# Which engine forms the low parts in the run-up to sparse attention, and when the compressed values of that layer are formed

## The chip, the cores and the metric

The kernel runs on one core of a Trainium2 chip. The metric is the device time of one execution in microseconds (us). Before the change the median of three runs is 1415.6 us (1414.58 to 1415.69). The trace comes from one more execution, which took 1416.84 us and whose span, from its first to its last instruction, is 1415.1 us.

## The reference, cut to what matters

The program is a two-layer decoder trunk over 512 tokens of width 1024. Layer 0 mixes retention and mLSTM heads. Layer 1 is a sparse-attention mixer. Each layer is followed by a gated feed-forward part and by an embedding of its own that is gated and added. Only the mixer of layer 1 matters here:

```
z = (h @ w_in).astype(jnp.float32)
q, kc, vc, ks, vs, kw, vw, gt = split_cols(z, NSA_SIZES)
q = rms_norm(q.reshape(B, T, G, HG, HD), q_g).transpose(0, 2, 3, 1, 4)
...
def compress(t, pos, w1, w2):
    blk = kv(t)[:, cidx] + pos[:, None, :]
    blk = blk.transpose(0, 3, 1, 2, 4).reshape(B, G, nc, CMP_BLOCK * HD)
    return jax.nn.gelu(blk @ w1) @ w2

kc = rms_norm(compress(kc, pos_k, w1k, w2k), k_g[0])
vc = compress(vc, pos_v, w1v, w2v)
```

There are 16 query heads of width 64. Keys and values are compressed in overlapping blocks of 32 tokens by a two-layer network: w1 (2048 to 256), a gelu, then w2 (256 to 64). "The second layer of the compressed values" is the product with w2 for the values. Scores against the compressed keys, against the selected blocks and against the window are then turned into probabilities, and their products with the values are added with gates. The layer's embedding `p @ ple_w` doesn't depend on the mixer and is worked in among the attention steps.

## The kernel before, in words

**Products in three pieces.** Every product of f32 data is done with each operand split into a high and a low part. ScalarE (ACT) copies the source to the high part (line 133), another engine subtracts it from the source for the low part (line 134), and TensorE (PE) runs three matmuls into one accumulator: high by high (L152), high by low (L153 or L154) and low by high (L154 or L153).

**Weights.** `load` (line 136) brings in one weight tile of 128x1024 f32, 512 KB. SyncE (SP) issues its DMA into `wr`, ACT forms `wh`, and either VectorE (DVE) or GpSimd (POOL) forms `wl`. Which of the two is read off the string `lo_seq`: "v" is DVE, "g" is POOL, and after each load the string is rotated by one letter, so that "vg" alternates. `wr`, `wh` and `wl` have three buffers each, so the fourth tile after a given one takes over its buffers once it is used up. `load` runs with a raised priority (`AHEAD` = 500 places), so the planner puts a tile's DMA, its `wh` and its `wl` far ahead of their place in the program.

**Order.** A planner goes over the traced program and writes one fixed queue for each engine from priorities and modelled costs. On the chip each engine works its queue in order, and semaphores hold an instruction until its inputs are there. Nothing overtakes on an engine.

**The run-up to attention**, from line 958 on, in program order: `thin` (two tiles w_cmp, the sum of squares and the scale of the norm), `kv` (four tiles w_kv), `blocks` and `kv_evac` (keys and values out of PSUM, the norm of the keys on DVE, their gains on POOL at L701), `hidden(0)` (four tiles w1, matmuls L745, L746 and L748), the first half of the queries `q0` (four tiles w_q, 24 three-piece matmuls each) with `key_stack` in between (transposes L714), the second layer of the compressed keys, `q_norm` of the first query halves on DVE (L818 to L831), `hidden(1)`, `q1` (four tiles w_q), and between the third and fourth tile of `q1` first `cmp_values(second(1, ...))` and then four `q_stack` (16 transposes at L838). After the fourth tile come four more `q_stack`, then `cmp_scores` (L858 to L870), and then the attention loop. That makes 22 loads: 2 + 4 + 4 + 4 + 4 + 4, and "vg" gives 11 of them to POOL.

**The attention loop** runs scores (L899 to L901), the maximum on DVE (L902), the exponential on ACT (L904), the division and gate on POOL (L909), transposes (L921) and products with the values (L931 to L943). Other work is hung into its steps: the embedding of the layer (`Embed.step`, three loads: pT and the first half of w_ple at m = 0, the second half at m = 4), the second half of the queries' norm on POOL, and the first half of the output projection (four loads of w_nso). `lo_seq` is "g" for all seven loads, so POOL forms 18 low parts in this layer's mixer.

`cmp_values` writes `vc`, which the first product at L931 reads. It takes two copies of 64 columns on ACT (L802), two subtractions on DVE (L803) and two products of 128x512 on DVE (L805). `second(1)` takes 12 matmuls of 128x64 (lines 152 to 154).

Of the kernel before, what the change touches and what calls it, by code (L numbers as in the profile page):

```python
# [60 lines left out]
class Trunk:  # L61
# [553 lines left out]
    def nsa_mixer(self):  # L615
# [4 lines left out]
        with ExitStack() as ctx:  # L620
# [134 lines left out]
            def hidden_t(hid, times):  # L755
                pt = self.ps("b")
                for q in range(2):
                    nc.tensor.transpose(pt[:, 64 * q : 64 * q + 64], hid[0:64, P * q : P * q + P], self.ident[0:64, 0:64])
                hh, hl = [self.y()[:, 0 : P * times].rearrange("p (x r b) -> p x r b", x=4, b=32) for _ in range(2)]
                self.split(hh, hl, pt[:, 0:P].rearrange("p (x b) -> p x b", x=4).unsqueeze(2).to_broadcast([P, 4, times, 32]))  # L760
                return hh, hl


            def second(which, hh, hl):
                po = self.ps("o")
                for g in range(1 + which):
                    out = po[:, 64 * g : 64 * g + 64] if which else po[0:64, 0:64]
                    for q in range(2):
                        ws = slice(P * which + 64 * q, P * which + 64 * q + 64)
                        xs = slice(2 * q + g, 2 * q + g + 2 - which)  # L770
                        ah, al = [x[:, xs].rearrange("p x r b -> p (x r b)") for x in (hh, hl)]
                        self.mm3(out, ah, al, w2[:, 0, ws], w2[:, 1, ws], q == 0, q == 1)
                return po
# [24 lines left out]
            def cmp_values(po):  # L798
                tmp = self.sc()
                for g in range(2):  # L800
                    hi, lo = tmp[:, P * g : P * g + 64], tmp[:, P * g + 64 : P * g + P]
                    nc.scalar.activation(hi.bitcast(F32R), po[:, 64 * g : 64 * g + 64], AF.Copy)  # L802
                    nc.vector.tensor_tensor(lo, po[:, 64 * g : 64 * g + 64], hi, ALU.subtract)  # L803
                    both = tmp[:, P * g : P * g + P].unsqueeze(1).to_broadcast([P, 4, P])
                    nc.vector.tensor_tensor(vc[g], both, rows4.unsqueeze(2).to_broadcast([P, 4, P]), ALU.mult)  # L805
# [29 lines left out]
            def q_stack(sts, hd):  # L835
                pk = self.ps("b")
                for t in range(NTT):
                    nc.tensor.transpose(pk[:, t * P : (t + 1) * P], sts[t][hd // 4][:, hd % 4].bitcast(F32).rearrange("p a d -> p (a d)"), self.ident)  # L838
                q = self.y()
                if hd % 2:  # L840
                    nc.vector.tensor_copy(q, pk)
                else:
                    nc.scalar.activation(q, pk, AF.Copy)
                return q


            def cmp_scores(g, qs):
                es = []
                for jp in range(2):
                    e = self.sc()  # L850
                    e4 = e.rearrange("p (j h n) -> p j h n", j=2, h=8)
                    e3 = e.rearrange("p (h n) -> p h n", n=32)
                    mx, sm = self.small(16), self.small(16)
                    for jj in range(2):
                        j = 2 * jp + jj
                        ps = self.ps("b").rearrange("p (h a n) -> p h a n", h=8, a=2)
                        for q in range(8):
                            nc.tensor.matmul(ps[:, q], qs[q][:, j * P : (j + 1) * P], kc[:, :, 32 * g : 32 * g + 32], start=True, stop=True)  # L858
                        nc.vector.tensor_tensor(e4[:, jj], ps[:, :, 0], maskc[:, j].unsqueeze(1).to_broadcast([P, 8, 32]), ALU.add)
                        nc.vector.tensor_tensor(e4[:, jj], e4[:, jj], ps[:, :, 1], ALU.add)  # L860
                    nc.vector.tensor_reduce(mx, e3, AX, ALU.max)
                    nc.gpsimd.tensor_tensor(e3, e3, mx.unsqueeze(2).to_broadcast([P, 16, 32]), ALU.subtract)
                    nc.scalar.activation(e, e, AF.Exp)
                    nc.vector.tensor_reduce(sm, e3, AX, ALU.add)
                    nc.vector.reciprocal(sm, sm)
                    sm3 = sm.rearrange("p (j h) -> p j h", j=2)
                    nc.vector.tensor_tensor(sm3, sm3, gate[:, 2 * jp : 2 * jp + 2, 8 * g : 8 * g + 8, 0], ALU.mult)
                    if jp == 0:
                        nc.vector.tensor_scalar(sm[:, 0:8], sm[:, 0:8], valid, None, ALU.mult)
                    nc.gpsimd.tensor_tensor(e3, e3, sm.unsqueeze(2).to_broadcast([P, 16, 32]), ALU.mult)  # L870
                    es.append(e)
                return es
# [82 lines left out]
                    outs[g][0].append(hi)  # L955
                    outs[g][1].append(lo)

            self.lo_seq = "vg"
            w2r = self.sc()
            nc.sync.dma_start(w2r[:, 0:256], I["w2"])  # L960
            w2 = np_.tile([P, 2, 256], F32R, name="w2")
# [27 lines left out]
            hvt = hidden_t(hv, 4)  # L989
            cmp_keys_t(st)  # L990
            q1.steps(2, 3)
            cmp_values(second(1, *hvt))
            qs = [q_stack(sts, hd) for hd in range(4)]
            q1.steps(3, 4)
            qs += [q_stack(sts, hd) for hd in range(4, 8)]
            ess = [cmp_scores(0, qs), None]
            self.lo_seq = "g"
            sts1 = []
            zq = [q_copy(q1.ps[0:2], 0), q_copy(q1.ps[2:4], 2)]

# [7 lines left out]
            emb = self.Embed(self, 1, lambda m: self.y().bitcast(F32))  # L1008

            def embed(m):  # L1010
                return lambda: emb.step(m)

            def more_q(lo, hi):
                def run():
# [18 lines left out]

            hooks[3] = [set_probs(0)]
            at("embed", [embed(m) for m in range(KD)])
            at("q_stack", [more_q(2 * i, 2 * i + 2) for i in range(4)])
            at("q_norm", [lambda i=i: q_norm(zq[i], sts1, nc.gpsimd) for i in range(2)])
# [241 lines left out]
```

## Time and profile before

| | |
|---|---|
| median of three runs | 1415.6 us |
| the profiled execution | 1416.84 us, span 1415.1 us |
| PE matmul busy | 1374.4 us, 97% |
| DVE busy | 847.2 us, 60% |
| ACT busy | 637.9 us, 45% |
| POOL busy | 383.2 us, 27% |
| mean granted clock of PE | 0.992 |

An engine's busy time is the time in which it has an instruction in work. A granted clock of 1.00 is 2.4 GHz and 0.5 is 1.2 GHz. A row of the waits says which instruction waited for which, how long in total, how often and at most. In the timelines a row is the start, the duration, the engine, the line, the operation and what it writes and reads. What stands in brackets is the engine's idle time before the instruction and what ended it. Matmuls overlap in the pipeline, so the rate is read from start to start and not from their durations.

### The profile page before, as it was taken

The numbers are of one execution on the slowest core, as the hardware profiler recorded it, in microseconds if no ns is written. First come the engines' busy times: TensorE is split into PE (matmuls) and PEld (weight loads), VectorE is DVE, ScalarE is ACT, GpSimd is POOL, SyncE is SP. The second block draws the span as 40 slices with busy tenths as digits, with TensorE's granted clock in tenths as the row PEclk, the third lists the DMA queues.
The fourth block names the chain that finished last, engine by engine and source line by source line (L and its number), as shares of the span: only waits on it lengthen the run. The fifth ranks groups of instructions, "written<-read, shape, count | busy, mean of one in ns | idle before, by whom it ended". The sixth has DMA issues, their size and how long they took to land.

```text
span 1415.1 us, 17986 instructions
## 1 busy us (share of the span) xinstructions
PE 1374.4 (97%) x6726; PEld 1127.8 (80%) x6726; DVE 847.2 (60%) x1368; ACT 637.9 (45%) x1121; POOL 383.2 (27%) x361
## 2 busy tenths in 40 slices
PE   9999999999999999999988899999999999999998
PEld 7778778888888888887766777777888888888887
DVE  6665656565356435577827798777575437534555
ACT  5257426444134223444443787777444224323341
POOL 4466102122041001123233675544222013100120
PEclk9999999999999999999999999999999999999999
DMA  6433323223323333333323110010233323333232
GB/s 215 129 114 92 112 79 107 90 91 104 94 85 105 104 89 93 96 118 96 106 88 119 31 31 30 16 46 5 86 104 98 96 90 105 94 100 94 84 106 75
DMA packets 40031, 127.96 MB, mean 90 GB/s; under 512 B 4740, under 2 KB 5380, under 8 KB 39944
## 3 DMA queue, kind: packets, MB, share of 16 engines
q1 hardware_dynamic: 39656, 126.68, 29.1%
q8 instruction: 53, 0.87, 0.3%
q14 instruction: 34, 0.28, 0.1%
q10 hardware_dynamic: 288, 0.14, 0.0%
HBM read 122.60 MB, written 3.15 MB: 89 GB/s over the span
## 4 chain that ended last, share of the span: by engine, by line
PE 82%; DVE 7%; ACT 3%; issue 3%; POOL 2%; POOLq 0%; ACTq 0%; DVEq 0%
PE ps L153 25%; PE ps L152 25%; PE ps L154 25%; PE ps L921 2%; PE ps L943 2%; ACT pr L904 1%; PE ps L363 1%; ACT pt L133 1%; DVE nmx L902 1%; DVE wl L134 1%; PE ps L900 1%; PE ps L899 1%; DVE pt L134 1%; PE ps L421 1%; DVE tiny L186 1%
## 5 line engine op out<-in xcount | busy, mean ns | idle before, releaser
L152 PE MATMUL ps<-y,wh 128*128 128x512 f32 (+1 forms) x1112 | 434.8, 391 | 3.3 <-ACT y L206 2.2
L153 PE MATMUL ps<-y,wh 128*128 128x512 f32 (+1 forms) x1112 | 432.1, 389 | 0.6 <-POOL y L134 0.6
L154 PE MATMUL ps<-y,wl 128*128 128x512 f32 (+1 forms) x1112 | 431.8, 389 | 0.0
L133 ACT ACTIVATE wh<-wr 128x1024 fp32r<-128x1024 f32 (+2 forms) x223 | 230.0, 1036 | 427.8 <-PE ps L153 347.4
L134 DVE TENSOR_TENSOR wl<-wr,wh 128x1024 fp32r<-128x1024 f32 (+2 forms) x185 | 226.8, 1228 | 48.3 <-ACT wh L133 47.8
L152 PEld LDWEIGHTS ps<-y,wh 128*128 128x128 f32 x1112 | 209.3, 188 | 47.4 <-ACT y L206 2.6
L153 PEld LDWEIGHTS ps<-y,wh 128*128 128x128 f32 x1112 | 209.3, 188 | 43.4 <-POOL y L134 1.1
L154 PEld LDWEIGHTS ps<-y,wl 128*128 128x128 f32 x1112 | 209.1, 188 | 43.3 <-DVE wl L134 0.2
L1082 POOL TENSOR_TENSOR sc<-sc,rb 128x512 f32<-128x512 f32 x44 | 56.9, 1293 | 476.7 <-ACT sc L1081 476.7
L152 PE MATMUL ps<-gh,wh 128*128 128x512 f32 x352 | 136.9, 389 | 0.0
L153 PE MATMUL ps<-gl,wh 128*128 128x512 f32 x352 | 136.9, 389 | 0.0
L154 PE MATMUL ps<-gh,wl 128*128 128x512 f32 x352 | 136.9, 389 | 0.0
L200 POOL TENSOR_TENSOR acc<-acc,sc 128x512 f32<-128x512 f32 x48 | 74.4, 1551 | 218.3 <-ACT sc L198 215.4
L134 POOL TENSOR_TENSOR wl<-wr,wh 128x1024 fp32r<-128x1024 f32 x36 | 88.1, 2449 | 160.9 <-ACT wh L133 140.5
L1097 DVE TENSOR_TENSOR hp<-hp,ps 128x512 f32<-128x512 f32 x48 | 33.0, 687 | 130.4 <-PE ps L154 130.4
L909 POOL TENSOR_SCALAR pr<-pr,sm,gate 128x512 f32<-128x512 f32 (+3 forms) x128 | 77.3, 615 | 65.5 <-DVE sm L907 45.8
L1083 DVE TENSOR_TENSOR sc<-ps,sc 128x512 f32<-128x512 f32 x44 | 30.4, 692 | 92.7 <-POOL sc L1082 83.5
L1075 DVE TENSOR_TENSOR a<-ps,rb 128x512 f32<-128x512 f32 x44 | 30.4, 690 | 91.8 <-PE ps L154 88.9
L152 PEld LDWEIGHTS ps<-gh,wh 128*128 128x128 f32 x352 | 66.1, 188 | 13.8
L153 PEld LDWEIGHTS ps<-gl,wh 128*128 128x128 f32 x352 | 66.1, 188 | 13.7
L154 PEld LDWEIGHTS ps<-gh,wl 128*128 128x128 f32 x352 | 66.1, 188 | 13.6
L1081 ACT ACTIVATE sc<-sc 128x512 f32<-128x512 f32 x44 | 27.8, 632 | 101.3 <-DVE sc L1080 101.3
(284 smaller groups left out, 2038.9 us busy)
## 6 DMA issues: line engine op xcount, KB each, us to landing
wr<-in_w_up_dram SPq DMA_DIRECT2D x88, 512.0 KB, 3.6
wr<-in_w_down_dram SPq DMA_DIRECT2D x32, 512.0 KB, 3.5
wr<-in_w_plg_dram SPq DMA_DIRECT2D x16, 512.0 KB, 3.7
wr<-in_w_down_dram SPq DMA_DIRECT2D x16, 384.0 KB, 3.1
hp<-in_xT_dram SPq DMA_DIRECT2D x16, 256.0 KB, 3.9
wr<-in_w_abo_dram SPq DMA_DIRECT2D x8, 512.0 KB, 3.6
wr<-in_w_dram SPq DMA_DIRECT2D x8, 512.0 KB, 3.7
wr<-in_w_q_dram SPq DMA_DIRECT2D x8, 512.0 KB, 3.7
```

What stands on the lines that cost most here:

```text
L133: self.nc.scalar.activation(hi, src, AF.Copy)
L134: (eng or self.nc.vector).tensor_tensor(lo, src, hi.bitcast(F32), ALU.subtract)
L152: mm(out, ah, bh, start=first, stop=False)
L153: mm(out, ah, bl, start=False, stop=False)
L154: mm(out, al, bh, start=False, stop=last)
L200: eng.tensor_tensor(n.acc, n.acc, sq, ALU.add)
L909: nc.gpsimd.tensor_scalar(prs[b], prs[b], sm[:, b : b + 1], gate[:, j, hd, 1 + b : 2 + b], ALU.mult, ALU.mult)
L921: nc.tensor.transpose(pb[:, i * P : (i + 1) * P], pr[:, n, i * P : (i + 1) * P], self.ident)
L1075: nc.vector.tensor_tensor(a, pa, n.b, ALU.mult)
L1082: nc.gpsimd.tensor_tensor(c, c, n.b, ALU.mult)
L1083: nc.vector.tensor_tensor(c, pb, c, ALU.mult)
L1097: nc.vector.tensor_tensor(self.h[m], self.h[m], ps, ALU.add)
```

## The change

Three edits, all in `nsa_mixer`:

- `lo_seq` starts as "v" and not as "vg".
- `cmp_values(second(1, *hvt))` moves from behind `q1.steps(2, 3)` to behind `q1.steps(3, 4)`, that is behind the first four `q_stack` and the matmuls of the last query tile. No DMA is moved with it: w2 is loaded at line 960.
- `lo_seq = "g"` is no longer set ahead of the attention loop but in the hook that runs `emb.step(4)`, behind it. The three loads of the embedding are thereby "v", and the four of w_nso, which come at step 60 and later, stay "g".

Of the 18 low parts on POOL, 14 go to DVE (11 of the run-up, 3 of the embedding) and 4 stay.

```
-            self.lo_seq = "vg"
+            self.lo_seq = "v"
...
             q1.steps(2, 3)
-            cmp_values(second(1, *hvt))
             qs = [q_stack(sts, hd) for hd in range(4)]
             q1.steps(3, 4)
+            cmp_values(second(1, *hvt))
             qs += [q_stack(sts, hd) for hd in range(4, 8)]
             ess = [cmp_scores(0, qs), None]
-            self.lo_seq = "g"
...
             def embed(m):
-                return lambda: emb.step(m)
+                def run():
+                    emb.step(m)
+                    if m == 4:
+                        self.lo_seq = "g"
+                return run
```

## Rows read from the trace of the kernel before

**Rows 1.** Waits of PE, 640 to 800 us: total us, times, longest.
```profile
PE ps L153 <- POOL wl L134: 4.5, 1, 4.5
PE ps L152 <- ACT y L133: 3.3, 1, 3.3
PE ps L745 <- POOL wl L134: 2.8, 2, 1.7
...
PE ps L234 <- DVE tiny L188: 2.2, 1, 2.2
```

**Rows 2.** Busy time of each engine by stretch, with granted clock, DMA share, GB/s.
```profile
700.00:780.00 80.00, 67.59 (x330) 55.23 (x329) 44.51 (x103) 35.22 (x68) 29.98 (x22) 0.91 0.34 106
780.00:800.00 20.00, 18.16 (x115) 14.66 (x114) 16.82 (x38) 13.54 (x32) 13.98 (x14) 1.00 0.10 27
```

**Rows 3.** Timeline of PE, 711 to 723 us.
```profile
716.18 0.80 PE L153 MATMUL ps<-wl,y 128*128 128x512 f32 x1 [4.50 <-POOL wl L134]
...
722.59 0.40 PE L153 MATMUL ps<-wl,y 128*128 128x512 f32 x1
722.82 0.40 PE L154 MATMUL ps<-wh,y 128*128 128x512 f32 x1
```

**Rows 4.** Timeline of POOL, 660 to 800 us, and its low parts together (duration min/median/max).
```profile
L134 POOL TENSOR_TENSOR wl<-wr,wh x18: 2333/2392/3111, 650.0 to 909.7; 128x1024 fp32r<-128x1024 f32 x18
...
697.05 1.76 POOL L690 TENSOR_TENSOR sc<-sc 128x256 f32<-128x256 f32 x3
700.50 1.29 POOL L690 TENSOR_TENSOR sc<-sc 128x256 f32<-128x256 f32 x1 [1.68 <-ACT sc L685]
...
708.59 5.23 POOL L701 TENSOR_TENSOR sc<-sc,gains 128x128 f32<-128x128 f32 x8 [4.48 <-DVE sc L699]
...
761.51 2.39 POOL L134 TENSOR_TENSOR wl<-wr,wh 128x1024 fp32r<-128x1024 f32 x1 [5.15 <-ACT wh L133]
```

**Rows 5.** Timeline of ACT at the second query tile.
```profile
707.36 2.00 ACT L133 ACTIVATE wh<-wr 128x1024 fp32r<-128x1024 f32 x2
```

**Rows 6.** Timeline of DVE, 660 to 800 us.
```profile
669.13 2.35 DVE L183 TENSOR_SCALAR tiny<-tiny 128x4 int32<-128x4 int32 x1
671.51 0.17 DVE L184 TENSOR_SCALAR tiny<-tiny 128x4 int32<-128x4 int32 x1
...
700.09 1.23 DVE L134 TENSOR_TENSOR wl<-wr,wh 128x1024 fp32r<-128x1024 f32 x1
...
709.38 0.68 DVE L699 TENSOR_TENSOR sc<-sc,tiny 128x256 f32<-128x256 f32 x1
...
736.68 0.69 DVE L818 TENSOR_TENSOR sc<-ep 128x512 f32<-128x512 f32 x1 [7.32 <-ACT ep L811]
...
743.18 2.58 DVE L818 TENSOR_TENSOR sc<-ep 128x512 f32<-128x512 f32 x1
...
747.54 2.72 DVE L818 TENSOR_TENSOR sc<-ep 128x512 f32<-128x512 f32 x1
...
754.02 2.35 DVE L186 TENSOR_TENSOR tiny<-tiny 64x1 f32<-64x1 f32 x1
...
761.59 2.34 DVE L186 TENSOR_TENSOR tiny<-tiny 128x16 f32<-128x16 f32 x1
...
766.44 1.42 DVE L831 TENSOR_TENSOR y<-ep,y 128x256 fp32r<-128x256 f32 x4
...
771.44 0.69 DVE L805 TENSOR_TENSOR vc<-sc,rows 128x512 fp32r<-128x512 f32 x1
```

**Rows 7.** Timeline of PE, 767 to 786 us.
```profile
767.82 0.42 PE L152 MATMUL ps<-w,y 128*128 128x64 f32 x1 [3.32 <-ACT y L133]
...
770.70 3.36 PE L838 MATMUL ps<-ident,y 128*128 128x128 f32 x16
...
779.36 1.47 PE L838 MATMUL ps<-ident,y 128*128 128x128 f32 x12
...
781.62 3.89 PE L858 MATMUL ps<-kc,y 128*128 128x64 f32 x32
```

## The prediction

> **What bounds the kernel now.** The page comes first: PE's matmuls fill 97% of the span, no other engine more than 60%, so time can only be won where PE stands still or runs at its lower clock. The waits of PE come second, and there the run-up to the attention of layer 1 stands out: from 640 to 800 us PE waits 4.5 us once and 2.8 us in two pieces (1.7 the longer) for a low part from POOL, 3.3 us for an ACT copy and 2.2 us for the small DVE steps of the norm [rows 1], together 12.8. The windows come third: between 700 and 780 us PE is busy 67.6 of 80 us and its granted clock is 0.91, while DVE is busy 44.5 us and POOL 30.0 [rows 2]. So the last 80 us of the run-up alone hold 12.4 us of idle PE and a few us of half clock. The timelines come last, and show what stands behind each wait.
>
> Two things are to be seen in them. First, POOL's low part for the second query tile sits in POOL's queue behind eight gain products, 5.23 us from 708.59 [rows 4], though its high part was there at about 708.4 (two high parts in 2.00 us from 707.36 [rows 5]). PE waits 4.50 us for it, and then runs at the lower of its two levels: from 716.18 to 722.59 there are 15 matmul starts in 6.41 us, at the later step of 0.23 us they would take 3.45 [rows 3]. That wait costs 4.50 + 2.96 = 7.46 us.
>
> Second, POOL's low parts hold up DVE. Small DVE steps that take 0.17 us take 2.35 (669.13), 2.35 (754.02) and 2.34 us (761.59), and squares that take 0.69 us take 2.58 (743.18) and 2.72 us (747.54) [rows 6]. Each begins beside one of POOL's low parts of 2.39 us and ends with it, the one at 761.59 for instance with the one of 761.51 [rows 4]. A low part that takes POOL 2.39 us takes DVE 1.23 [rows 4, 6], and where it would also have held DVE up, moving it to DVE makes DVE's work shorter.
>
> **The change part by part.** Every gain or loss is against the profiled execution.
>
> *(a) The norm's chain.* PE waits 2.2 us for the norm's chain [rows 1], which lost 2.35 - 0.17 = 2.18 us to POOL [rows 6]. If the moved low part goes into the chain, DVE gets back 2.18 - 1.23 = 0.95 us; behind the chain, PE gets back all 2.2. I take -1.3, near the lower end, because the raised priority puts a low part where its high part is ready.
>
> *(b) The w1 tiles.* Of the 2.8 us [rows 1], DVE needs 1.23 where POOL needs 2.39, twice 1.16 at best, and a place in DVE's queue. -1.6, with ends 0 and -2.8.
>
> *(c) The second query tile.* With its high part at 708.4, DVE could have the low part at 709.6, or, behind the four products of which the last begins at 709.38 and takes 0.68 [rows 6], at 711.3. PE asked for it at 716.18 - 4.50 = 711.7. Either way nothing is waited for, and the clock has no reason to fall: -7.0, leaving 0.5 for a PE that arrives earlier. Ends -7.5 and -4.0, where a shorter wait still brings the lower clock.
>
> *(d) DVE from 740 us to the query stacks.* The four stalls there are 1.89, 2.03, 2.18 and 2.17 us, together 8.3 [rows 6]. In their place come the low parts of four tiles, 4 x 1.23 = 4.9. DVE ends the norm of the query halves 3.4 us earlier against the start of the stretch, so at 764.5 and not 767.86 (766.44 + 1.42 [rows 6]). PE, done with the third query tile at 767.82 - 3.32 = 764.5 before [rows 7], would be there at about 763 after the 1.6 us of (b).
>
> *(e) The move of the second layer.* Before, PE waits 3.32 us for its input at 767.82 and then runs it and 16 transposes at the lower clock: 2.88 us for 12 small matmuls, which at the 0.12 us of L858 (3.89 us for 32) would be 1.46, and 3.36 us for 16 transposes, which at 1.47 us for 12 would be 1.96 [rows 7]. That is 3.32 + 1.42 + 1.40 = 6.1 us. After the move, its input is late by a tile's 24 matmuls (24 x 0.23 = 5.5 us) and can't be waited for. What is late next is the query stacks, whose inputs come from (d) at 764.5, while PE is there at 763. If the planner has the last tile's matmuls ahead of them, all 6.1 us go; if not, 1.5 us of wait remain, and perhaps the lower clock. I take -4.5, ends -6.1 and -1.5. The move issues no DMA, but its two copies on ACT and its four DVE steps go with it. Their reader, the first product with the compressed values, comes six steps into the attention loop (`LAG` + `VALUES_LAG`), so their results are not late.
>
> *(f) What DVE gets at the start of attention.* Between 780 and 800 us DVE is busy 16.8 of 20 us and PE 18.2 [rows 2]. There the change puts the second layer's two products of 0.69 us [rows 6] with two short subtractions (1.8 us), and the third embedding tile's low part (1.23). +2.0, ends 0 and +3.0.
>
> *(g) The rest.* The low parts of other tiles (three in `kv` and w1, the last one or two of `q0`, two of the embedding) fall where PE has a tile in hand, 5.5 us of matmuls for 1.23 us of DVE: 0. If that cover were gone, each would cost up to 1.23. DMA: the buffers of a tile come free 1.16 us earlier, which helps if anything. POOL loses 14 x 2.39 = 33 us of work, and its other work there isn't what PE waits for.
>
> The Trainium skill ("SBUF — State Buffer", Who interferes with whom) speaks against expecting too much. Row first: one POOL square takes 1.29 us at 700.50 while a DVE low part of 1.23 us runs from 700.09; three before it take 1.76 together, 0.59 each [rows 4, 6]. The rule says that a DVE instruction with two inputs in SBUF and a POOL instruction that reads SBUF exclude each other, and whichever issues first holds the other up. By it the change turns the blocking round, 14 times up to 1.23 us on POOL, where before it was 2.39 on DVE; the trace agrees, with 0.70 us lost in that row. It would leave the sum as it is, since POOL has 50 of 80 us free, and it adds to the first rival.
>
> The sum: -1.3 - 1.6 - 7.0 - 4.5 + 2.0 = -12.4, with (d) inside (e). 1416.84 - 12.4 = 1404.4 for an execution like the profiled one, which was 1.24 us over the median of the three runs; so 1403.2. The ends together: -2.2 - 2.8 - 7.5 - 6.1 = -18.6 (1397.0), and -0.95 - 0 - 4.0 - 1.5 + 3.0 = -3.5 (1412.1).
>
> **The rivals.**
>
> *First: the gains are passed on as waits of the attention.* (a) to (c) hold, but the stacks stay ahead of the last query tile, and DVE, which is full from 780 on, gives back what PE wins: -1.0 - 1.0 - 6.5 - 1.5 + 3.0 = -7.0, some 1408.6. For it: the 16.8 of 20 us [rows 2]. Against it: DVE starts that stretch with less behind it.
>
> *Second: the planner's new order eats the gain.* All queues from 640 us on are written anew. If the long wait only moves to another tile, so that -7.0 becomes -2 and the rest nets out against (f), it is 1413 to 1416, within a hair of before. For it: a queue in which nothing overtakes, as at 708.59 [rows 4]. Against it: DVE's low part is half as long, and DVE is idle 35 of 80 us [rows 2].
>
> *Third, slower: DVE becomes the bound from 740 to 800 us.* If DVE's stalls belong to what else runs on POOL there, or come back as waits behind instructions that wait for ACT, the 4.9 us of (d) are added to DVE's chain and not taken out of 8.3. Its end moves from 767.86 to 772.8, PE goes on 5.0 us later than before, at the lower clock as before, and (f) takes its 3.0: +8.0, against -1.0 from (a) and -4.0 from (c), the lower ends. That is +3.0, so 1419.8 for the profiled execution and 1418.6 for the median. The point from which it is slower than before: a chain to the last L831 that is longer by 2.0 us (5.0 - 3.0). For it: DVE is busy 44.5 of 80 us already [rows 2]. Against it: five stalls that end with POOL's low part [rows 4, 6].
>
> **How the numbers follow.** The forecast, 1397 to 1407, gets 0.55; the first rival (1405 to 1412) 0.23; the second 0.09; the third 0.13. A measurement of this kernel can tell about 0.2% (2.8 us) from no change. Faster by more than that takes the forecast, the first rival and a little of the second: 0.79. Within: 0.08. Slower: 0.13. The range, 1395 to 1413, goes from 2 us below the lower end of the terms, for half-rate stretches that are not priced here, to the second rival's first us, and leaves out the third rival and part of the second.
>
> **What would show it.** For (c): no wait of PE for a low part above 1 us between 700 and 720, and a clock of 1.00 there. For the stalls: no DVE step of 0.17 us with 2.3 us up to the embedding. For (e): the last query tile's matmuls without a gap behind the third's, ahead of the second layer, and transposes at 0.11 us. For (f): the first transposes of the compressed probabilities (L880) later against the first scores than before. The attention loop should take as long as before. The prediction is wrong if PE's idle time between 640 and 800 doesn't shrink by 6 us or more, or if it does and the loop gets longer by as much.

## The result, and the profile after

The change makes the kernel faster: 1397.78 us (median of 4 runs, 1397.32 to 1399.21) against 1415.34 (median of 4), a ratio of 0.9878 with a 95% interval of 0.9861 to 0.9895. Forecast were 1403.2 us and a range of 1395 to 1413; the gain is 17.6 us where 12.4 were worked out. The profiled execution took 1398.08 us (span 1396.3), 18.8 less than that of before. These are the busy times of its engines over the whole span.

```profile
PE 1369.7 (98%) x6726; PEld 1123.2 (80%) x6726; DVE 850.2 (61%) x1382; ACT 638.8 (46%) x1121; POOL 348.8 (25%) x347
```

DVE did 14 more low parts (14 x 1.23 = 17.2 us), yet its busy time grew by only 3.0 us, from 847.2 to 850.2. So, as an estimate, some 14 us of what counted as busy before was time in which DVE instructions stood still.

The waits of PE from 640 to 800 us (total us, times, longest) answer to [rows 1]. The 4.5, 3.3, 2.8 and 2.2 us of before are gone, and one wait at the start of the attention is now the longest (1.7 us before).

```profile
PE ps L880 <- POOL sc L870: 2.3, 1, 2.3
...
PE ps L152 <- ACT y L206: 0.6, 1, 0.6
...
PE ps L745 <- DVE wl L134: 0.4, 2, 0.2
```

The windows answer to [rows 2]: start and end, length, busy time (and count) of PE, weight load, DVE, ACT and POOL, then granted clock, DMA share and GB/s. Up to 762 us PE is busy for all but 2.1 of 122 us, at a clock of 1.00 and 0.99. Then comes an 18 us stretch with a clock of 0.76.

```profile
640.00:700.00 60.00, 59.23 (x279) 47.45 (x279) 46.47 (x82) 29.86 (x45) 12.21 (x10) 1.00 0.37 113
700.00:762.00 62.00, 60.68 (x333) 50.29 (x331) 43.74 (x109) 34.10 (x65) 8.92 (x15) 0.99 0.40 127
762.00:780.00 18.00, 15.71 (x66) 12.20 (x67) 12.58 (x30) 9.28 (x23) 8.78 (x11) 0.76 0.00 0
780.00:800.00 20.00, 18.05 (x112) 12.98 (x112) 16.37 (x40) 17.24 (x49) 14.06 (x16) 1.00 0.17 53
```

DVE's timeline (start, duration, instruction) answers to [rows 6]. Line 1159 is line 1156 of before, where this instruction took 2.48 us; the step at 666.41 took 2.35, the squares (L818) 2.58 and 2.72. All have their short times now. A low part at 667.10 sits right behind the norm's short steps.

```profile
650.02 0.75 DVE L1159 SCALAR_TENSOR_TENSOR sc<-ep,cols,sc 128x512 f32<-128x512 f32 x1
...
666.41 0.17 DVE L183 TENSOR_SCALAR tiny<-tiny 128x4 int32<-128x4 int32 x1
...
667.10 1.23 DVE L134 TENSOR_TENSOR wl<-wr,wh 128x1024 fp32r<-128x1024 f32 x1
...
730.33 0.67 DVE L818 TENSOR_TENSOR sc<-ep 128x512 f32<-128x512 f32 x1
...
749.53 1.42 DVE L831 TENSOR_TENSOR y<-ep,y 128x256 fp32r<-128x256 f32 x4
...
779.24 2.39 DVE L188 SCALAR_TENSOR_TENSOR tiny<-tiny,tiny 128x16 f32<-128x16 f32 x1
```

Of single DVE instructions of over 2 us, eight start between 640 and 800 before, and one after. That last one, at 779.24, begins beside the first low part that stayed on POOL (w_nso) and ends with it, as POOL's timeline shows; the eight gain products (L701, [rows 4]) now have nothing behind them that PE waits for.

```profile
702.65 4.87 POOL L701 TENSOR_TENSOR sc<-sc,gains 128x128 f32<-128x128 f32 x8 [7.38 <-DVE sc L699]
...
779.20 2.40 POOL L134 TENSOR_TENSOR wl<-wr,wh 128x1024 fp32r<-128x1024 f32 x1 [0.94 <-ACT wh L133]
```

PE's timeline at the place of the move answers to [rows 7]. The second layer (128x64, from 754.39) waits for nothing. The third query tile ends at 747.07. Behind it the planner has four transposes of the stacks (L838, 746.91) and 11 matmuls of the last query tile, and then mixes the next transposes with the rest of that tile; before, the second layer stood directly behind the third tile.

```profile
746.91 0.60 PE L838 MATMUL ps<-ident,y 128*128 128x128 f32 x4
...
754.39 0.19 PE L152 MATMUL ps<-w,y 128*128 128x64 f32 x1
...
755.64 2.00 PE L838 MATMUL ps<-ident,y 128*128 128x128 f32 x16
757.69 2.87 PE L858 MATMUL ps<-kc,y 128*128 128x64 f32 x24
760.39 0.66 PE L899 MATMUL ps<-hp,y 128*128 128x512 f32 x1
...
772.84 0.66 PE L880 MATMUL ps<-ident,sc 128*128 128x128 f32 x4 [2.29 <-POOL sc L870]
```

Where the time came from can be read from the start of four matmuls that both kernels have (the first of L672, behind the first norm; the last of L746, the first layer of w1; the first of L880, the first transpose of the compressed probabilities; the last of L943, the attention's last product):

| | before | after | gained since the row above |
|---|---|---|---|
| L619, first DMA of this layer | 624.7 | 623.6 | 1.1 (ahead of the changed stretch) |
| L672 | 698.8 | 692.3 | 5.4 |
| L746 | 746.1 | 729.6 | 10.0 |
| L880 | 792.7 | 772.8 | 3.4 |
| L943 | 980.4 | 962.0 | -1.5 |
| end of span | 1415.1 | 1396.3 | 0.4 |

The 1.1 us on top are not the change's: the clock between 40 and 100 us was 0.97 in the one execution and 1.00 in the other.

### The profile page after: what moved, and what is told of

Its sections match the earlier page's. It is cut to its first block, busy times and chain, and to the rows that moved or that the text cites. A ratio compares the mean times of both kernels' runs of the same rounds, so it can differ in the third digit from the quotient of the medians.

```text
span 1396.3 us, 17997 instructions
## 1 busy us (share of the span) xinstructions
PE 1369.7 (98%) x6726; PEld 1123.2 (80%) x6726; DVE 850.2 (61%) x1382; ACT 638.8 (46%) x1121; POOL 348.8 (25%) x347
## 4 chain that ended last, share of the span: by engine, by line
PE 82%; DVE 4%; issue 4%; ACT 4%; POOL 2%; DMA 0%; POOLq 0%; DVEq 0%; ACTq 0%
PE ps L152 25%; PE ps L153 25%; PE ps L154 25%; PE ps L943 2%; PE ps L921 1%; ACT pr L904 1%; DVE nmx L902 1%; ACT pt L133 1%; DVE wl L134 1%; PE ps L363 1%; DVE pt L134 1%; PE ps L899 1%; PE ps L900 1%; PE ps L421 1%; POOL acc L200 1%
## 5 line engine op out<-in xcount | busy, mean ns | idle before, releaser
L134 DVE TENSOR_TENSOR wl<-wr,wh 128x1024 fp32r<-128x1024 f32 (+2 forms) x199 | 244.9, 1233 | 43.2 <-ACT wh L133 42.2
L904 ACT ACTIVATE pr<-ps,nmx 128x512 f32<-128x512 f32 (+3 forms) x128 | 67.2, 533 | 9.4 <-DVE nmx L902 6.0
```

What stands on the lines that cost most here:

```text
L134: (eng or self.nc.vector).tensor_tensor(lo, src, hi.bitcast(F32), ALU.subtract)
L904: nc.scalar.activation(pr[:, b], s[:, b], AF.Exp, bias=nmx[:, b : b + 1], accum_out=sm[:, bs[b] : bs[b] + 1])
```

## The experiments

Ratios are to the kernel before, run beside each on the same chip, with the 95% interval.

**The run-up's low parts alone.** The kernel before with one edit.

```
-            self.lo_seq = "vg"
+            self.lo_seq = "v"
```

> Only the 11 low parts of the run-up go to DVE; the second layer stays in its place and the embedding's low parts stay on POOL. Theory (direct waits for POOL's low parts, and DVE held up beside them): nearly the whole gain, 12 to 16 us of 17.6, the wait of 4.5 us gone. Rival (the move carries a third of the gain): 9 to 12 us, with a wait and half clock left at the second layer.

Measured: 1400.89 us, before beside it 1415.81; ratio 0.9889 (0.9876 to 0.9902). These 11 low parts bring 14.9 us, nearly all of the gain, and the first L672 and the last L746 start within 0.4 us of the whole change (691.9 and 729.2). Behind them two of the embedding's low parts on POOL still hold up DVE. These are DVE's and POOL's timelines of this kernel:

```profile
741.25 3.50 DVE L825 TENSOR_TENSOR ep<-ep,tiny 128x512 f32<-128x512 f32 x2
...
750.83 2.72 DVE L831 TENSOR_TENSOR y<-ep,y 128x256 fp32r<-128x256 f32 x2 [0.77 <-ACT y L830]
```

```profile
741.48 2.72 POOL L134 TENSOR_TENSOR wl<-wr,wh 128x1024 fp32r<-128x1024 f32 x1 [27.75 <-ACT wh L133]
750.57 2.36 POOL L134 TENSOR_TENSOR wl<-wr,wh 128x1024 fp32r<-128x1024 f32 x1 [6.36 <-ACT wh L133]
```

PE waits twice for DVE's differences for the query stacks (L831), and the clock falls. Only the second wait belongs to a stop of DVE, the one at 750.83. The first L831 that PE waits for ends 2.8 us behind the third query tile (749.73 and 746.92), as in the changed kernel (2.9), but there 11 matmuls of the last query tile stand ahead of the transposes that read it, and here the planner has one. PE's timeline and the window:

```profile
747.11 0.48 PE L152 MATMUL ps<-wh,y 128*128 128x512 f32 x1
749.78 0.44 PE L838 MATMUL ps<-ident,y 128*128 128x128 f32 x2 [2.19 <-DVE y L831]
...
753.26 0.69 PE L838 MATMUL ps<-ident,y 128*128 128x128 f32 x2 [1.05 <-DVE y L831]
```

```profile
740.00:760.00 20.00, 16.25 (x67) 13.33 (x68) 15.03 (x37) 7.96 (x19) 5.08 (x2) 0.76 0.22 70
```

**The move alone.** The kernel before with the second layer moved.

```
-            cmp_values(second(1, *hvt))
             qs = [q_stack(sts, hd) for hd in range(4)]
             q1.steps(3, 4)
+            cmp_values(second(1, *hvt))
```

> Only the second layer moves; all 18 low parts stay on POOL. By the prediction's term (e) the move brings 4.5 us by itself, as the wait of 3.3 us and the half clock behind it go. Rival: without the low parts on DVE the query stacks are as late as before, PE waits for them instead, and the move brings 0 to 2 us. The 4.5 us wait for the second query tile's low part stays in both.

Measured: 1418.27 us; ratio 1.0019 (1.0010 to 1.0027). The move alone costs 2.5 us. The 3.3 us wait of the second layer is gone, and one of 2.2 us stands at the query stacks, as PE's timeline shows; the wait of 4.5 us stays.

```profile
765.53 0.33 PE L838 MATMUL ps<-ident,y 128*128 128x128 f32 x1 [2.20 <-DVE y L831]
```

With the low parts still on POOL, DVE's chain to the last L831 ends at 766.48 (765.06 + 1.42), 3.4 us behind the third query tile (763.11), just as before (767.86 and 764.50). The planner puts two transposes and then this wait directly behind that tile, and all 24 matmuls of the last tile come after it. So the move by itself doesn't bring the order that the changed kernel has.

**All but the move.** The changed kernel with the second layer back at its old place.

```
             q1.steps(2, 3)
+            cmp_values(second(1, *hvt))
             qs = [q_stack(sts, hd) for hd in range(4)]
             q1.steps(3, 4)
-            cmp_values(second(1, *hvt))
```

> All 14 low parts on DVE, the second layer in its old place. If the move is worth 4.5 us, this is 4 to 5 us slower than the whole change; if the planner mixes the last query tile in by itself once DVE has the low parts, it is within 1.5 us of it.

Measured: 1395.21 us (1393.81 to 1398.11); ratio 0.9858 (0.9844 to 0.9873). Without the move the kernel is as fast as with it or faster by 2.6 us; the intervals of the two ratios overlap, so the sign is not settled, but a gain of 4.5 from the move is excluded. The wait of 3.3 us goes without the move too, and not because its input comes much sooner. Before, the input is a copy that ACT makes behind four L830, which wait for DVE; it ends at 767.76 (767.19 + 0.57), 3.3 us behind the third query tile (764.50). ACT's timeline of the kernel before:

```profile
765.95 1.33 ACT L830 ACTIVATE y<-ep 128x256 fp32r<-128x256 f32 x4 [4.22 <-DVE ep L825]
767.19 0.57 ACT L133 ACTIVATE y<-ps 128x512 fp32r<-128x512 f32 x1
```

In this kernel the same copy ends at 750.24 (749.67 + 0.57), still 2.9 us behind the third tile (747.39). What fills these 2.9 us is the planner's new order: four transposes and 11 matmuls of the last query tile stand ahead of the second layer (128x64), which starts at 750.30 with no wait. ACT's and PE's timelines of this kernel, and the window behind, which keeps the full clock:

```profile
749.67 0.57 ACT L133 ACTIVATE y<-ps 128x512 fp32r<-128x512 f32 x1
```

```profile
747.00 0.39 PE L154 MATMUL ps<-wh,y 128*128 128x512 f32 x1
747.23 0.60 PE L838 MATMUL ps<-ident,y 128*128 128x128 f32 x4
...
749.98 0.39 PE L153 MATMUL ps<-wl,y 128*128 128x512 f32 x1
750.30 0.30 PE L152 MATMUL ps<-w,y 128*128 128x64 f32 x1
```

```profile
760.00:800.00 40.00, 34.22 (x211) 25.92 (x211) 34.97 (x85) 28.02 (x78) 26.87 (x31) 1.00 0.17 53
```

Against the run-up alone (1400.89, same chip) the embedding's three low parts bring 5.7 us here. Two things come with them, two stops of DVE less and that order, and no run takes them apart.

**POOL's reads put back beside DVE's work.** The changed kernel, and for each of the 14 moved low parts a further POOL instruction of the same shape, which reads the high part twice and writes scratch that nothing reads.

```
+            self.dum = np_.tile([P, 1024], BF16, name="dum")
...
+            if self.dup[0] == "y":
+                nc.gpsimd.tensor_tensor(self.dum, hi.bitcast(F32), hi.bitcast(F32), ALU.subtract)
+            self.dup = self.dup[1:] + self.dup[0]
```

> The whole change, and beside each of the 14 low parts that went to DVE an instruction of the same shape on POOL that reads the high part twice and writes a scratch tile nobody reads (extra work, the outputs are untouched). Queues of the other engines are the same, nobody waits for the extra work. Theory (POOL's instruction holds DVE up): small DVE steps of 0.17 us take 2.3 again, and the time goes up by 5 to 9 us. Rival (only the wait for POOL's result counted): within 1.5 us of the whole change.

Measured: 1421.11 us; ratio 1.0039 (1.0027 to 1.0051): 23.3 us over the changed kernel by the medians, far more than the 5 to 9 of the theory, though nothing waits for the scratch. In DVE's and POOL's timelines (lines stand 5 lower here) a square of 0.67 us takes 2.15, and a short step 1.85; the short step ends with POOL's instruction (755.60 + 1.85 = 757.45, and 754.78 + 2.66 = 757.44).

```profile
749.12 2.15 DVE L823 TENSOR_TENSOR sc<-ep 128x512 f32<-128x512 f32 x1
...
755.60 1.85 DVE L192 SCALAR_TENSOR_TENSOR tiny<-tiny,tiny 64x1 f32<-64x1 f32 x1
```

```profile
748.83 1.89 POOL L150 TENSOR_TENSOR dum<-wh 128x1024 bf16<-128x1024 f32 x1 [1.49 <-ACT wh L134]
754.78 2.66 POOL L150 TENSOR_TENSOR dum<-wh 128x1024 bf16<-128x1024 f32 x1 [4.06 <-ACT wh L134]
```

PE's queue around the stacks has the order of the changed kernel (four transposes and 11 matmuls of the last tile behind the third), and yet PE waits 1.7 us there for L831: with DVE held up, that order isn't enough.

The added instruction starts on the same high part as DVE's own low part and so meets it more often than the low parts of before did; that it ends above the kernel before is no measure of what these cost there.

**The same time on POOL without the reads.** As the last, but the added work reads two columns and then writes the scratch twice.

```
+                nc.gpsimd.tensor_tensor(self.dum[:, 0:2], hi[:, 0:2].bitcast(F32), hi[:, 0:2].bitcast(F32), ALU.subtract)
+                for _ in range(2):
+                    nc.gpsimd.memset(self.dum, 0.0)
```

> As e6_dup, but the extra work on POOL only writes: after a two-column trigger it fills the scratch tile twice by memset (extra work, the outputs are untouched). Theory (DVE is held up because POOL reads SBUF beside it): the steps of DVE stay short and the time within 3 us of the whole change. Rival (what counts is that POOL is busy and its own work late): as slow as e6_dup, 1416 to 1421.

Measured: 1403.46 us, before beside it 1416.87; ratio 0.9904 (0.9889 to 0.9919). From 640 to 1010 us POOL is busy 179.4 us here and 176.4 in the last kernel, so it is as full, and yet the time is 17.7 us lower by the medians (19.1 by the ratios). What differs is that the added work hardly reads, and that it comes in two pieces of 0.95 us. DVE's instructions with two inputs keep their times beside these pieces too (last section), so the difference is put to POOL's reads beside DVE. Against the changed kernel 5.7 us remain by the medians (3.7 by the ratios), some more than the 3 of the theory. The longest new row in the waits of PE is for a POOL cast (L715) that comes late behind the added writes; smaller ones stand beside it, and how the rest divides isn't shown.

```profile
PE ps L721 <- POOL st L715: 2.9, 1, 2.9
```

The Trainium skill ("SBUF — State Buffer", Who interferes with whom) has the same division: by it a DVE instruction with two inputs in SBUF contends with a POOL instruction that reads SBUF, and not with one that only writes. The trace agrees: of single DVE instructions over 2 us between 640 and 800 there are nine in the kernel with the added reads, each beside one of them (four are DVE's own low parts, of 2.9 us), and one in the kernel with the added writes, at 785.54, beside a w_nso low part on POOL, which reads.

**One tile of the second query product.** The kernel before with the low part of only that tile on DVE, which PE waited 4.5 us for.

```
-            self.lo_seq = "vg"
+            self.lo_seq = "vgvgvgvgvgvvvgvgvgvgvg"
```

> The kernel before with one low part of the 22 on the other engine: that of the second query tile, on DVE. Theory: the wait of 4.5 us and the 15 matmuls at half clock go, 6 to 7.5 us faster than before. Rival: the wait moves to the next of POOL's low parts (the fourth query tile), 1 to 3 us faster.

Measured: 1409.20 us, before beside it 1415.03; ratio 0.9951 (0.9938 to 0.9965), 5.8 us from one instruction, a little under the 6 to 7.5 of the theory. The 4.5 us wait is gone from the list, and the others stand.

```profile
PE ps L745 <- POOL wl L134: 3.0, 2, 1.7
PE ps L152 <- ACT y L133: 2.9, 1, 2.9
PE ps L152 <- ACT y L206: 2.2, 1, 2.2
PE ps L234 <- DVE tiny L188: 2.2, 1, 2.2
```

**The first two.** The kernel before with the two low parts ahead of the first norm on DVE.

```
-            self.lo_seq = "vg"
+            self.lo_seq = "vvvvvgvgvgvgvgvgvgvgvg"
```

> The kernel before with the low parts of the second w_cmp and the second w_kv tile on DVE. Prediction's term (a): 1.3 us. What the trace after suggests: both stalls of DVE there (at the end of the layer before and in the norm's chain) go, with the half clock behind, 4 to 5.5 us.

Measured: 1410.07 us; ratio 0.9965 (0.9951 to 0.9979), 5.0 us. L672 starts at 691.9, as early as with all of them. In the waits of PE the one for the norm's steps (L234) is gone, and the one for ACT's copy (L206) is down from 2.2 to 0.6 us:

```profile
PE ps L152 <- ACT y L206: 0.6, 1, 0.6
```

**The embedding alone.** The kernel before with only the embedding's three low parts on DVE.

```
-            self.lo_seq = "g"
+            self.lo_seq = "v"
...
+                    if m == 4:
+                        self.lo_seq = "g"
```

> The kernel before with the three low parts of the embedding on DVE; the run-up keeps its 11 on POOL and the second layer its place. If each low part that leaves POOL is worth what it held up, whatever the others do: 4 to 6 us faster, as much as lies between e1_runup and e3_no_move. If the embedding's only count once the run-up is tight (DVE then gets to the query stacks last): 0 to 2.5 us faster, with the second layer's wait of 3.3 us shorter and the 4.5 us wait as before.

Measured: 1420.04 us, before beside it 1417.18; ratio 1.0022 (1.0013 to 1.0032), 3 us slower, which neither expectation had. The edit that brings 5.7 us on top of the run-up costs something by itself. PE's order at the second layer is that of the kernel before, with a wait of 2.9 us there (3.3 before). The attention starts 1.4 us earlier (L899 at 779.2), but at a lower clock than the 1.00 of [rows 2], and the first L880 comes 2.4 us later than before (795.1 against 792.7).

```profile
780.00:800.00 20.00, 17.70 (x85) 14.49 (x85) 14.65 (x34) 9.00 (x21) 7.41 (x9) 0.74 0.09 27
```

**The second layer later still.** The changed kernel with the second layer in the attention loop.

```
-            cmp_values(second(1, *hvt))
...
+            hooks[2] = [lambda: cmp_values(second(1, *hvt))]
```

> The whole change, with the second layer of the compressed values still later, in the third step of the attention loop. Theory: PE's clock fell at 760 us after a long row of small matmuls (12 of the second layer, 16 transposes, 24 scores); with the 12 taken out it stays at 1.00 and 2 to 3 us more are won. Rival: the clock falls anyway, and the 12 matmuls and 4 DVE steps come in the way of the loop: 0 to 2 us slower than the whole change.

Measured: 1397.71 us; ratio 0.9877 (0.9861 to 0.9893), the same as the changed kernel. The clock doesn't fall at 760 any more (it falls at 775 and 850), and the wait of L880 for POOL is 4.5 us in two pieces instead of 2.3. What the one gives, the other takes, or neither weighs much: the run doesn't tell.

**The second layer done twice.** The kernel without the move, with the 12 small matmuls of the second layer run a second time, their result unused, at the place that the change gives them.

```
             q1.steps(3, 4)
+            second(1, *hvt)
```

> As e3_no_move, with the 12 matmuls of the second layer run a second time where the change puts them; nobody reads the second result (extra work, the outputs are untouched; 12 matmuls take about 1.3 us at full clock). Theory (a longer row of small matmuls ahead of the attention lets PE's clock fall): the granted clock falls at about 760 us and it is 3 to 5 us slower than e3_no_move. Rival (the four DVE steps of the move cost the time): 0.5 to 1.5 us slower, no fall of the clock there.

Measured: 1396.58 us; ratio 0.9858 (0.9842 to 0.9875), 1.4 us over the kernel without the move by the medians and nothing by the ratios. The small matmuls at that place cost no more than their own time. The clock falls at 760 here too (0.81 and 0.51 in two windows of 5 us).

**All 18 on DVE.** The changed kernel with w_nso's four low parts on DVE as well, and then the same without the move. The edit of both, and the second's in addition:

```
-                def run():
-                    emb.step(m)
-                    if m == 4:
-                        self.lo_seq = "g"
-                return run
+                return lambda: emb.step(m)
```

```
+            cmp_values(second(1, *hvt))
             qs = [q_stack(sts, hd) for hd in range(4)]
             q1.steps(3, 4)
-            cmp_values(second(1, *hvt))
```

> The whole change, and the four low parts of the first half of the output projection on DVE as well. If POOL's low part costs wherever DVE has small steps beside it (2.39 us in one step at 779), 1 to 3 us faster than the whole change. Rival: in the loop DVE is full, 4 x 1.23 us more on it cost 1 to 4 us.

> All low parts of the mixer of layer 1 on DVE (18 of 18), the second layer in its old place: the two steps that were faster than the whole change, 2.6 and 2.0 us, taken together. If they add up: 1393 us, 22 to 23 us under the kernel before. If DVE is full in the loop once the stretch ahead of it is tight: 1395 or more.

Measured: 1395.79 us, ratio 0.9861 (0.9848 to 0.9875); and 1395.48 us, before beside it 1416.87, ratio 0.9851 (0.9837 to 0.9866). Both are as fast as the kernel without the move (1395.21), and the three can't be told apart; the two steps don't add up to the 1393 us expected. They are the fastest found, some 2 us below the change, by a difference that their intervals don't separate from it.

## Why the prediction was right, and where it was off

The sign, the range and two reasons held: PE's waits for POOL's low parts, and DVE instructions that POOL's low parts hold up, were what could be won at the norm, the w1 tiles and the second query tile. At the stacks a third came in, the planner's new order of PE's work, which the prediction saw only as a condition of the move. By parts the medians give 14.9 for the run-up, 5.7 for the embedding and -2.6 for the move, 18.0 in all, where the change as a whole measured 17.6. The time lies near the lower end of the forecast because (a) and the embedding were worth more than forecast and the move nothing; that the stretch of (e) still gained 3.4 us is luck as far as (e) goes, since another edit brought it.

**(a), the norm's chain: -1.3, too small.** The two low parts ahead of it bring 5.0 us by themselves, and the trace 5.4 up to L672. The term counted the norm's step and its 2.2 us wait only. It left out the low part at 650, which held DVE's L1156 for 2.48 us; with that gone, PE's wait for ACT's copy behind it (L206) went from 2.2 to 0.6 us. That wait had its row in the same list as [rows 1], and the prediction passed over it. The waits of PE, DVE's and POOL's timelines of the kernel before:

```profile
PE ps L152 <- ACT y L206: 2.2, 1, 2.2
```

```profile
650.50 2.48 DVE L1156 SCALAR_TENSOR_TENSOR sc<-ep,cols,sc 128x512 f32<-128x512 f32 x1 [0.74 <-ACT sc L1155]
```

```profile
650.03 2.40 POOL L134 TENSOR_TENSOR wl<-wr,wh 128x1024 fp32r<-128x1024 f32 x1 [36.70 <-ACT wh L133]
```

The rest is the clock: before, the two windows of 5 us from 670 have a clock of 0.96 and 0.70, after it is 0.99 or more in both. And the norm lost its whole wait, not the lower end, since the low part came behind its short steps (667.10).

**(b) and (c): -1.6 and -7.0, right in sum.** Together they were 8.6, and the stretch between L672 and L746 gained 10.0. The single tile of (c) measured 5.8 us, between the ends of 4.0 and 7.5; no wait of PE for a low part over 0.4 us is left, and the clock is back at 1.00 around 715. The half-rate matmuls behind the wait went with it, as worked out from [rows 3].

**(d), DVE from 740 us on: the stalls went, the gain did not come.** The stalls at the squares and the small steps are gone from 640 to 762 us, and DVE ends the last stack's difference at 750.95 (749.53 + 1.42) where it was 767.86: 16.9 us earlier, of which 16.5 were gained already at L746. That is 0.4 us for this stretch, where 3.4 were worked out. In DVE's queue there stand five more low parts and not four (the fifth, at 748.40, is the embedding's). PE ends the third query tile 3.9 us before DVE's end, where it was 3.4 before and 1.5 in the prediction. So there the low parts cost DVE nothing net, and bring it next to nothing.

**(e), the move: -4.5, wrong.** This is the step that failed. It made the order in which the last query tile covers the wait an effect of the move. The runs put that order to the low parts on DVE, the embedding's among them: without the move the planner has 11 matmuls of the last tile ahead of the second layer, and the 3.3 us of wait and the lower clock behind it are gone; with the move alone they are not ahead of the stacks, PE waits 2.2 us there, and the time is 2.5 us longer. Nor did the input come much earlier against PE's work: ACT's copy ends 2.9 us behind the third tile in both kernels with the 14 low parts on DVE (749.93 and 747.07 with the move), and 3.3 before. The prediction named the order as a condition ("If the planner has the last tile's matmuls ahead of them"), and gave the gain to the wrong one of the two edits. The gain of 3.4 us between L746 and L880 belongs to the low parts, and the kernel without the move has 6.3 there ((792.7 - 770.1) - (746.1 - 729.8)). Why the planner mixes the tiles in only then is not shown.

**(f), the attention's start: +2.0, about right.** L880 waits 2.3 us for POOL and not 1.7, it comes 12.4 us behind the first score (L899) where it was 12.2, and from L880 to the last L943 the attention takes 189.2 us where it took 187.7. The first rival, gains passed on as waits of the attention, is in these 1.5 us and the 0.6 of L880, and goes no further.

**(g), the rest: 0, wrong for the embedding.** Its low parts were costed at nothing because PE had a tile in hand. On top of the run-up they bring 5.7 us: on POOL they stop DVE twice at the stacks, and the planner has one matmul of the last tile there and not 11. The prediction had one of these stalls in (d), the one at 761.59, but not that it stays if only the run-up's low parts move.

The third rival, DVE as the bound, did not come: POOL's part of the stalls was real, as the two kernels with added work on POOL show. The second rival, an order that eats the gain, did not come either: the planner's new order covers the wait at the stacks.

What stays open: how much of the gain at the stacks is the order and how much DVE's stops (the added reads show that the order alone isn't enough), and why the embedding's low parts alone cost 3 us. For the latter the trace has the lower clock at the attention's start and the later L880, and no run takes that clock away by itself. Whether the move costs anything in the changed kernel is not settled either (the clock, in the last section, may be all of it).

## What to carry to other kernels

When two engines share a kind of work, price it on each as its own time plus the time for which it stops the other: here a POOL instruction of 2.4 us held up DVE steps of 0.17 us, and giving DVE 14 more instructions added 3 us to its busy time. A wait that names a third engine (ACT's copy, here) may still come from such a stop two steps earlier; follow it back before calling it untouched. And when two edits aim at the same wait, run each alone: here the one that was meant to change the order only moved the wait, and the other removed it through the order that the planner made of it. To see which it was, measure how late the input is against the work in front of it, and count what stands between.

## What was not expected of the hardware

- The clock falls without an idle PE ahead of it, and the order of PE's work alone doesn't say when. After the change no wait stands in PE's timeline from 746.91 to 760.39; in the last 6.0 us there are only small matmuls (12 of the second layer, 16 transposes, 24 of L858), and then the granted clock falls to 0.55. These are two windows of 5 us of the changed kernel, and then the second of them in the one with all 18 on DVE and no move:

```profile
755.00:760.00 5.00, 4.95 (x45) 4.66 (x44) 4.33 (x9) 3.95 (x7) 0.00 (x0) 1.00 0.31 104
760.00:765.00 5.00, 5.00 (x21) 4.11 (x21) 4.08 (x10) 1.41 (x3) 1.05 (x1) 0.55 0.02 6
```

```profile
760.00:765.00 5.00, 5.00 (x24) 4.15 (x24) 4.38 (x11) 1.61 (x4) 1.05 (x1) 0.62 0.28 103
```

  The latter kernel has the PE order of the kernel without the move, up to the small matmuls and to 0.3 us, and yet its clock falls where that one's stays at 1.00. In both the first L880 comes 2.7 us later than there (772.8 and 772.7 against 770.1). Executions of one kernel differ as well: the four of the kernel without the move took 1393.8 us twice, at a mean clock of 0.998, and 1396.6 and 1398.1 at 0.996 and 0.995. So the 2.6 us between the change and the kernel without the move may be this fall, and not the move.
- A POOL instruction that only writes held up DVE too, once. In the kernel with the added writes an int32 step of DVE that takes 0.16 us took 0.91, beside the first of two memsets; between 738 and 760 us the DVE instructions with two inputs kept their times beside such writes. The rows of DVE and of POOL:

```profile
744.09 0.91 DVE L190 TENSOR_SCALAR tiny<-tiny 128x16 int32<-128x16 int32 x1
```

```profile
744.02 1.96 POOL L152 MEMSET dum<- 128x1024 bf16 x2
```
- Two low parts on POOL that no wait of PE named were worth nearly as much as one that it waited 4.5 us for: the two ahead of the norm brought 5.0 us, the one of the second query tile 5.8.
